# A decoder layer on one core: an order table for attention, a transpose moved to the next half, tile addresses and late loads

## The chip, the cores and the metric

The kernel runs on one core of a Trainium2 chip. A core has five engines that run side by side, each through its own list of instructions in a fixed order: PE (TensorE, the matrix products), DVE (VectorE), ACT (ScalarE), POOL (GpSimd) and SP (SyncE, which only issues transfers here). They wait for each other by semaphores. The metric is the device time of one execution in microseconds (us), lower is better.

## What is computed

One layer for 512 tokens of width 1024, batch 1, in float32. The reference, cut to its skeleton:

```python
h = rmsnorm(x, norm_mix_pre)
z = h @ w_in                      # 1024 x 6704
xr, gr, q, kc, vc, ksl, vsl, kw, vw, g_nsa, gm_rnn, gm_attn = split(z)
y_rnn = rg_lru(causal_conv(xr), ...) * gelu(gr)
kc_c, vc_c = compress(kc, ...), compress(vc, ...)     # 31 blocks of 32 tokens
y_attn = g0 * o_cmp + g1 * o_slc + g2 * o_win         # 16 heads, 4 kv groups, causal, ALiBi
y = sigmoid(gm_rnn) * y_rnn + sigmoid(gm_attn) * y_attn
x = x + rmsnorm(y @ w_out, norm_mix_post)
gate, up = split(rmsnorm(x, norm_ffn_pre) @ ffn_w_gate_up)          # 2 x 2816
x = x + rmsnorm((silu(gate) * up) @ ffn_w_down, norm_ffn_post)
x = x + sigmoid(x @ ple_w_gate + ple_b_gate) * (p @ ple_w_proj)
```

With 512 tokens every block is selected and the window covers all, so the selected and the windowed branch are both full causal attention, with keys and values of their own (branch 0 and 1), beside the compressed branch with its 31 keys.

## The kernel before

Every product is made in three float32r products, high by high, high by low and low by high. A weight block comes by a transfer from SP into `raw`, ACT casts it to `wh`, DVE subtracts to get `wl`; the same is done for every activation (`aTh`, `aTl`) and for the attention weights (`PT`).

The program runs through these stages: the front (norm, transposes to `aTh`/`aTl`, values, the recurrent branch, compression; to about 190 us), attention (about 190 to 455 us), the output projection, the FFN's up part (from about 529 us), its down part, and at the end the gated input embedding (PLE, from about 859 us).

PE's instructions stand in program order. In attention that order is written out by hand. The heads go in eight pairs `p`, and a pair in two halves of the queries, run by `run(p, half, order)` with a string of letters: S a block of scores (PE, bank `sc`, then DVE reduces and copies it to `e` with its minimum `mn`, ACT takes the exponential, and after the last block of a row DVE works out `sm` and POOL scales `e` by it), T a transpose of `e` into a bank `tr` (then an ACT cast and a DVE subtraction make `PT`), M a product of `PT` with the values (bank `pv` in first halves, `mq` in second ones), C the same for the compressed branch. X, Y and Z are the compressed branch of one group of four heads, which is needed by two pairs: X its scores, Y its softmax (`cmp_soft`: DVE steps on `c` and `csm`, the exponential on ACT, and a last product `c*csm` on POOL, line 888), Z its turn (`cmp_turn`: four transposes of `c` into one bank `tr`, two casts `pc` on ACT, line 902, and two subtractions on DVE, line 904). X, Y and Z of the next group stand in the second half of odd pairs (`ODD`). There are two banks of each of `mm`, `sc` and `tr`, so a third user waits until the first one's readers are done.

Digits are fills: one fill is one step (three matmuls) of the projections that lie ready in `attn` (keys `k`, queries `q`, gates `rnn` and `att`). They are what PE does between the dependent steps; there are 224 of them, in one fixed row, and a job's readers on ACT and DVE run when its eighth step is done. `PRO` lists the fills between the steps of the start of attention, before the first pair: `PRO[0]` of them stand ahead of the first scores, `scores(0, 0, 0)`, and `PRO[5]` ahead of `cmp_turn(0)`. The first scores read `KS`, of which one half of the partitions comes by a transfer that POOL issues (line 750).

On the other engines a scheduler sets the order when the program is built, from its own estimate of when each instruction can start. So a change in PE's order changes theirs. `issue_after(x)` says that what is inside may not be put ahead of `x` on its own engine.

The other places: `norm1` takes the reciprocal root on POOL (line 231, a power of a column); POOL fills tables (`toep`, `ctab`, lines 464 to 473) and clears `KC`, `Vz` and `vct` (lines 508 to 510) early in the front, after the first power, `pow0`. In the FFN's up part `gu_act` (line 1157) reads the first product with SiLU into `st`, whose tiles, like `r`, `a` and `s`, come from the pool `ff` at the time of their first use. At the end, `ple_gate_load(ch, k2)` loads, casts and splits one of four blocks `wg` of the PLE gate's weight for one half `ch` of the columns (lines 1209 and 1210); those of `ch` 1 are issued before the third token tile of `ch` 0. Beside them `to_T` (lines 243 and 244) transposes `x1[0]` and `x1[1]` through four banks `sc` into `aTh` and `aTl`, in the middle of the second tile's products.

Of the kernel before, what the change touches and what calls it, by code (L numbers as in the profile page):

```python
# [8 lines left out]
F32 = mybir.dt.float32  # L9
# [7 lines left out]
S, D, KT, TT = 512, 1024, 8, 4  # L17
# [8 lines left out]


HALF0 = "S T S 1 S 2 S T 1 S 2 M S T 1 S T 1 S M M 1 M C 3"
EVEN = "1 T S T 1 C S M T 1 M T 1 S M T T 1 M 1 S T 1 M T 1 M 1 M 3 M"
ODD = "T T X 1 S M T C S 1 Y M S 1 T T M 1 S T M 1 T 2 T M Z M 2 M 1 M 1"  # L30
LAST = "T O O T 1 C 1 O 1 M O T T O O O M 2 M M T W 4 T 2 M T M 1 T 1 M 1 M"
PRO = (22, 5, 0, 2, 1, 10)
TK = (1, 7, 1)
TV = (12, 7, 8, 11)
VP = ()
# [3 lines left out]
def f32(ap):  # L39
    return ap.bitcast(F32)  # L40
# [3 lines left out]
def layer_kernel(ctx, tc, a, out):  # L44
    nc = tc.nc
# [13 lines left out]
    def nm(s):  # L59
        uid[0] += 1  # L60
        return f"{s}{uid[0]}"
# [164 lines left out]
    last = {}  # L226
# [28 lines left out]
    KC = mid.tile([128, NG, 32], F32, name="KC")  # L255
    Vz = mid.tile([128, NG, 2, 128], F32R, name="Vz")
# [3 lines left out]
    vct = mid.tile([64, NG, 4, 32], F32, name="vct")  # L260
# [134 lines left out]
    tp(pg[:, :KT], g_rows, ident[:KT, :KT])  # L395
    kept(nc.vector.tensor_copy(g_col, pg[:, :KT]))
    xn = norm1_halves(x0)
    pow0 = last["pow"].ins
    keep_warm(6)
    with tc.issue_after(last["xn"].ins):  # L400
        vw_first(0, 2, "a")
# [58 lines left out]


    late_pool = ctx.enter_context(ExitStack())
    late_pool.enter_context(tc.issue_after(pow0))
    nc.gpsimd.iota(toep, pattern=[[-1, S]], base=384, channel_multiplier=1,
                   allow_small_or_imprecise_dtypes=True)
    nc.gpsimd.affine_select(toep, toep, pattern=[[-1, S]], base=384, channel_multiplier=1,
# [38 lines left out]
    e2 = e2_stack.enter_context(tc.tile_pool(name="e2", bufs=2, reuse_waits="tile"))  # L505


    nc.gpsimd.memset(KC, 0.0)
    nc.gpsimd.memset(f32(Vz), 0.0)
    nc.gpsimd.memset(vct, 0.0)  # L510
    w2src = [a[n_][0].rearrange("(k p) d -> p k d", p=128) for n_ in ("cmp_k_w2", "cmp_v_w2")]
    for u in range(2):
        nc.sync.dma_start(w2k[:, :, u, :], w2src[0])
# [1 line left out]
    X2s, BLK, PM = {}, {}, {}  # L515
# [340 lines left out]
    def cmp_scores(g):  # L856
        p_ = bank("sc")
        for r in range(4):
            mm(p_[32 * r:32 * r + 32, :], KC[:, g, :], f32(QS[4 * g + r]), start=True, stop=True)
        s1 = ap_.tile([128, S], F32, tag="pvt", name=nm("c1"), bufs=1)  # L860
        nc.scalar.activation(s1, p_, AF.Copy, scale=slcol[:, g:g + 1])
        CG["s1"] = s1

    def cmp_soft(g):
        pt = bank("tr", [128, TT, 4, 32])
        s1 = CG.pop("s1")
        for i in range(TT):
            tp(pt[:, i].rearrange("p r c -> p (r c)"), s1[:, i * 128:(i + 1) * 128], ident)
        s2 = ap_.tile([128, TT, 4, 32], F32, tag="c2", name=nm("c2"), bufs=1)
        for r in range(4):  # L870
            nc.vector.scalar_tensor_tensor(s2[:, :, r, :], ctab, SLOPE[4 * g + r], pt[:, :, r, :],
                                           op0=OP.mult, op1=OP.add)
        mn = ap_.tile([128, TT, 4], F32, tag="cmn", name=nm("cmn"))
        nc.vector.tensor_reduce(mn, s2, axis=AX.X, op=OP.min)
        nc.vector.tensor_scalar(mn, mn, 1.0e30, None, op0=OP.min)
        s2f = s2.rearrange("p i r c -> p (i r) c")
        mnf = mn.rearrange("p i r -> p (i r)")
        nc.vector.tensor_sub(s2f, s2f, mnf[:, :, None].broadcast_to([128, 16, 32]))
        tt = tab if g == 0 else (lambda x: x)
        tt(nc.scalar.activation(s2, s2, AF.Exp, scale=-1.0))  # L880
        sm = ap_.tile([128, TT, 4], F32, tag="csm", name=nm("csm"))
        nc.vector.tensor_reduce(sm, s2, axis=AX.X, op=OP.add)
        nc.vector.tensor_scalar(sm, sm, 1.0e-30, None, op0=OP.max)
        nc.vector.reciprocal(sm, sm)
        gv = gates[:, :, 12 * g:12 * g + 12].rearrange("p i (r b) -> p i r b", b=3)
        nc.vector.tensor_mul(sm, sm, gv[:, :, :, 0])
        smf = sm.rearrange("p i r -> p (i r)")
        nc.gpsimd.tensor_mul(s2f, s2f, smf[:, :, None].broadcast_to([128, 16, 32]))
        CG["s2"] = s2

    def cmp_turn(g):
        pt2 = bank("tr")
        s2 = CG.pop("s2")
        for i in range(TT):
            tp(pt2[:, i * 128:(i + 1) * 128], s2[:, i].rearrange("p r c -> p (r c)"), ident)


        pc = ap_.tile([128, 2, S], F32R, tag="pc", name=nm("pc"), bufs=1)
        lo, hi = slice(0, 64), slice(64, 128)
        hl = list(enumerate(((lo, hi), (hi, lo))))  # L900
        for m, (h_, l_) in hl:
            nc.scalar.copy(pc[h_, m, :], pt2[h_, :])
        for m, (h_, l_) in hl:
            nc.vector.tensor_sub(pc[l_, m, :], pt2[h_, :], f32(pc[h_, m, :]))
        PTc[g] = pc
# [54 lines left out]
    def run(p, half, order):  # L960


        pv_open(p, half)
        if half == 0:
            ss = iter([(p, i, u, (br,)) for i in (2, 3) for u in range(2) for br in range(2)])
        else:
            ss = iter([(p + 1, i, u) for i in (0, 1) for u in range(2)])
        ts, ms, ys = (iter(range(n)) for n in (len(pv_steps(half)), len(pv_steps(half)), KT))
        g = p // 2 + 1
        do = {"S": lambda: scores(*next(ss)), "T": lambda: turn_step(p, half, next(ts)),  # L970
              "M": lambda: pv_step(p, half, next(ms)), "C": lambda: pv_cmp(p, half), "O": lambda: y_split(next(ys)),
              "W": lambda: split_out(), "X": lambda: cmp_scores(g), "Y": lambda: cmp_soft(g), "Z": lambda: cmp_turn(g)}
        for c in order.replace(" ", ""):
            if c.isdigit():
                fill(int(c))
            else:
                do[c]()
        pv_close(p, half)
# [4 lines left out]
    cmp_vz()  # L983
    fill(PRO[0] - 14)
    scores(0, 0, 0)
    fill(PRO[1])
    scores(0, 0, 1)
    fill(PRO[2])
    scores(0, 1, 0)
    fill(PRO[3])  # L990
    cmp_scores(0)
    scores(0, 1, 1)
    fill(PRO[4])
    cmp_soft(0)
    fill(PRO[5])
    cmp_turn(0)
    for p in range(KT - 1):
        run(p, 0, HALF0)
        run(p, 1, (EVEN, ODD)[p % 2])
    p = KT - 1  # L1000
    run(p, 0, HALF0)
# [6 lines left out]
    def split_out():  # L1008
        f_split(NJ + 3, out_hl)
# [131 lines left out]
    NJ2, HS = NF // 2, S // 2  # L1141
    BLK = [tuple(range(b, min(b + 2, NJ2))) for b in range(0, NJ2, 2)]
# [44 lines left out]
    lateb_stack.close()  # L1187
    wo_stack.close()
    ff = ctx.enter_context(tc.tile_pool(name="ff", bufs=1, reuse_waits="tile"))
    for f in range(2):  # L1190
        gu_act(f, *first[f][1])
    for f in range(2, NF):
# [39 lines left out]
    X, Y6, Y7, Z = ([bank(x), bank(y_)] for x, y_ in (("mm", "mm"), ("sc", "sc"), ("tr", "tr"), ("pv", "mq")))  # L1232
# [6 lines left out]
    for b, js in enumerate(BLK):  # L1239
        n = len(js)  # L1240
# [81 lines left out]
    def ple_gate_load(ch, k2):  # L1322
        raw = wraw(wpg[:, 2 * k2:2 * k2 + 2, ch * S:(ch + 1) * S], [128, 2, S], "f", 0)
        if ch == 0:
            hl = ff.tile([128, 2, 2, S], F32R, tag=f"r{k2}", name=nm("wg"))
            h, l = hl[:, 0], hl[:, 1]
        else:
            tags = ("a0", "a1", "a2", "a3", "a4", "s0", "s1", "s2")[2 * k2:2 * k2 + 2]
            h, l = (ff.tile([128, 2, S], F32R, tag=t_, name=nm("wg")) for t_ in tags)
        WG[ch, k2] = split(h, l, raw)  # L1330
# [32 lines left out]
    for ch in range(2):  # L1363
        for i, t in enumerate(ORDER):
            if ch == 0 and i == 2:
                for k2 in range(4):
                    ple_gate_load(1, k2)
            tl = slice(t * 128, (t + 1) * 128)
            pj = bank("tr")
            three(pj, [(pT[0][:, k, tl], pT[1][:, k, tl], WP[ch][0][:, k], WP[ch][1][:, k]) for k in range(2)])  # L1370
            end = ch == 1 and i == TT - 1
            for c0, n_ in ((0, S),) if not end else ((0, S // 2), (S // 2, S // 2)):
                p_ = bank("mm")[:, :n_]
                wc = slice(c0, c0 + n_)
                three(p_, [(aTh[:, k, tl], aTl[:, k, tl], WG[ch, k // 2][0][:, k % 2, wc], WG[ch, k // 2][1][:, k % 2, wc])
                           for k in range(KT)],
                      {1: lambda: to_T(x1[0], 0, "sc"), 5: lambda: to_T(x1[1], 1, "sc")} if (ch, i) == (0, 1) else {})
                z = ff.tile([128, 2, S], F32, tag="st", name=nm("z"), bufs=2)[:, 0, :n_]
                cs = slice(ch * S + c0, ch * S + c0 + n_)
                nc.vector.tensor_add(z, p_, b_g[:, cs])  # L1380
                tab(nc.scalar.activation(z, z, AF.Sigmoid))
                nc.vector.tensor_mul(z, z, pj[:, wc])
                nc.vector.tensor_add(z, z, x1[t][:, cs])
                nc.sync.dma_start(out[0, t * 128:(t + 1) * 128, cs], z)
# [30 lines left out]
```

## Time and profile before

| what | us |
|---|---|
| median of three runs | 927.18 |
| the three runs | 925.63 to 927.47 |
| profiled execution | 926.09 |
| its span in the trace | 924.3 |
| PE busy in it | 903.7 |
| DVE busy | 617.5 |
| ACT busy | 491.5 |
| POOL busy | 128.2 |

The profiled execution has its own time, 926.09 us. Its span, from the first to the last instruction of the trace, is 924.3 us, so 1.8 us lie around it. The engines run side by side, so their busy times overlap. [...]

Matmuls are pipelined: the trace gives one of 512 columns some 0.39 us, and the next starts about 0.23 us after it. PE's time is therefore read from the starts. In the order listings below a row is: the line of the code, the operation, output<-inputs, shape, and a repeat count. All lines after 29 are one higher in the changed kernel.

### The profile page before, as it was taken

The page shows a single profiled execution, that of the slowest core. Times are in us where ns is not written, and L with a number is a line of the kernel's source. Part 1 is how long each engine was busy: PE and PEld are TensorE (multiplying, and loading weights), DVE is VectorE, ACT ScalarE, POOL GpSimd, SP SyncE. Part 2 cuts the span into 40 slices and gives each one's busy share as a digit, 9 for nine tenths or more (in the row PEclk, how much of TensorE's full clock was granted, in tenths as well). Part 3 has the DMA queues.
Part 4 walks back from the last instruction along what each step waited for, and adds up shares of the span by engine and source line. Part 5 has one row for each costly group of instructions (what it writes and reads, how often), then busy time and mean ns, then how long its engine had stood idle before and what let it go on. Part 6 is the DMA issues. An engine that isn't in the chain of part 4 may idle for free.

```text
span 924.3 us, 12453 instructions
## 1 busy us (share of the span) xinstructions
PE 903.7 (98%) x4493; PEld 745.3 (81%) x4493; DVE 617.5 (67%) x1205; ACT 491.5 (53%) x898; POOL 128.2 (14%) x211
## 2 busy tenths in 40 slices
PE   7999999999999999999999999999999999999997
PEld 6978888867878878888888988888888888877786
DVE  6657886967788788886857444434333478898932
ACT  6468868656667667666744322223222245465600
POOL 3001202122243213233303000000000000000100
PEclk9999999999999999999999999999999999999999
DMA  9334345462123111201055123333333345626401
GB/s 298 87 91 114 101 118 147 99 106 66 50 60 78 46 47 46 69 30 62 27 200 160 55 83 91 102 104 91 92 104 101 91 138 186 200 93 224 151 35 46
DMA packets 124206, 94.58 MB, mean 102 GB/s; under 512 B 6168, under 2 KB 107376, under 8 KB 124144
## 3 DMA queue, kind: packets, MB, share of 16 engines
q1 hardware_dynamic: 122976, 91.68, 33.6%
q0 software_dynamic: 1152, 2.10, 1.5%
q8 instruction: 35, 0.57, 0.3%
q14 instruction: 27, 0.22, 0.1%
q10 hardware_dynamic: 16, 0.00, 0.0%
HBM read 89.58 MB, written 2.10 MB: 99 GB/s over the span
## 4 chain that ended last, share of the span: by engine, by line
PE 82%; DVE 9%; ACT 4%; DMA 3%; issue 2%; POOL 0%; SPq 0%; POOLq 0%; ACTq 0%; DVEq 0%
PE mm L96 42%; PE sc L96 24%; PE mq L96 5%; PE tr L96 4%; PE tr L99 4%; PE pv L96 4%; DVE wl L158 1%; DVE PT L923 1%; DMA x<-in_x_dram 1%; DMA KS<-KS 1%; DMA raw<-in_ple_w_gate_dram 1%; DVE aTl L1210 1%; DVE e L837 1%; ACT e L840 1%; DVE T L1222 1%
## 5 line engine op out<-in xcount | busy, mean ns | idle before, releaser
L96 PE MATMUL mm<-aTh,wh 128*128 128x512 f32 (+1 forms) x536 | 211.6, 395 | 0.6 <-ACT st L1157 0.6
L96 PE MATMUL mm<-aTl,wh 128*128 128x512 f32 (+1 forms) x536 | 206.1, 384 | 0.1
L96 PE MATMUL mm<-aTh,wl 128*128 128x512 f32 (+1 forms) x536 | 206.1, 384 | 0.0
L96 PEld LDWEIGHTS mm<-aTh,wl 128*128 128x128 f32 x536 | 100.7, 188 | 20.7
L96 PEld LDWEIGHTS mm<-aTh,wh 128*128 128x128 f32 x536 | 100.9, 188 | 20.2 <-issue 3.4
L84 ACT CAST wh<-raw 128x1024 fp32r<-128x1024 f32 x43 | 45.3, 1054 | 134.4 <-PE mm L96 58.3
L96 PEld LDWEIGHTS mm<-aTl,wh 128*128 128x128 f32 x536 | 101.0, 188 | 16.4 <-DVE aTl L244 0.5
L852 POOL TENSOR_SCALAR e<-e,sm 128x128 f32<-128x128 f32 (+3 forms) x128 | 79.2, 635 | 158.2 <-DVE sm L848 120.0
L85 DVE TENSOR_TENSOR wl<-raw,wh 128x1024 fp32r<-128x1024 f32 x43 | 52.6, 1224 | 67.3 <-ACT wh L84 62.7
L158 DVE TENSOR_TENSOR wl<-raw,wh 128x1024 fp32r<-128x1024 f32 x59 | 73.2, 1244 | 28.9 <-ACT wh L157 24.3
L840 ACT ACTIVATE e<-e,mn 128x128 f32<-128x128 f32 (+3 forms) x128 | 71.5, 560 | 31.3 <-DVE mn L837 20.4
L96 PE MATMUL sc<-aTh,wl 128*128 128x512 f32 (+1 forms) x208 | 79.3, 381 | 0.5 <-DVE wl L158 0.5
L96 PE MATMUL sc<-aTh,wh 128*128 128x512 f32 (+1 forms) x208 | 79.3, 381 | 0.0
L96 PE MATMUL sc<-aTl,wh 128*128 128x512 f32 (+1 forms) x208 | 79.2, 381 | 0.0
L157 ACT CAST wh<-raw 128x1024 fp32r<-128x1024 f32 x59 | 61.6, 1048 | 25.6 <-PE mm L96 20.9
L837 DVE CUSTOM_DVE_ANT_0 e<-sc,toep 128x128 f32<-128x128 f32 (+3 forms) x128 | 59.4, 482 | 19.2 <-PE sc L96 18.6
L923 DVE TENSOR_TENSOR PT<-tr,PT 128x512 fp32r<-128x512 f32 x96 | 56.6, 595 | 14.0 <-ACT PT L922 13.2
L922 ACT CAST PT<-tr 128x512 fp32r<-128x512 f32 x96 | 47.9, 512 | 24.9 <-PE tr L99 20.9
L1043 POOL TENSOR_TENSOR ss<-ss,ss 128x1 f32<-128x1 f32 x8 | 4.9, 615 | 388.0 <-ACT junk L1031 388.0
L96 PE MATMUL sc<-KS,QS 128*128 128x512 f32 (+2 forms) x192 | 54.3, 365 | 2.8 <-DMA KS<-KS 1.9
L99 PE MATMUL tr<-ident,e 128*128 128x128 f32 x320 | 48.5, 272 | 0.0
L99 PEld LDWEIGHTS tr<-ident,e 128*128 128x128 f32 x320 | 39.9, 140 | 8.8
(365 smaller groups left out, 1747.2 us busy)
## 6 DMA issues: line engine op xcount, KB each, us to landing
raw<-in_w_in_dram SPq DMA_DIRECT2D x48, 512.0 KB, 3.8
raw<-in_ffn_w_gate_up_dram SPq DMA_DIRECT2D x44, 512.0 KB, 3.8
raw<-in_ffn_w_down_dram SPq DMA_DIRECT2D x30, 512.0 KB, 4.3
raw<-in_ple_w_gate_dram SPq DMA_DIRECT2D x8, 512.0 KB, 4.1
x<-in_x_dram SPq DMA_DIRECT2D x7, 512.0 KB, 8.4
raw<-in_w_out_dram SPq DMA_DIRECT2D x6, 512.0 KB
raw<-in_cmp_k_w_dram SPq DMA_DIRECT2D x4, 512.0 KB, 3.7
raw<-in_cmp_v_w_dram SPq DMA_DIRECT2D x4, 512.0 KB, 3.9
```

What stands on the lines that cost most here:

```text
L84: nc.scalar.copy(h, raw)
L85: nc.vector.tensor_sub(l, raw, f32(h))
L96: return pe(nc.tensor.matmul(*args, **kw))
L99: return pe(nc.tensor.transpose(*args))
L157: nc.scalar.copy(h, RAW[n])
L158: nc.vector.tensor_sub(l, RAW[n], f32(h))
L837: nc.vector.tensor_tensor_reduce(e[:, br, :], src, toep[:, 384 - 128 * i:S], SLOPE[h], BIG, op0=OP.add, op1=OP.min, accum_out=mn[:, u, br: ...
L840: tt(nc.scalar.activation(e[:, br, :], e[:, br, :], AF.Exp, scale=-1.0, bias=mn[:, u, br:br + 1], accum_out=sm[:, u, br:br + 1]))
L852: nc.gpsimd.tensor_scalar(ev, ev, sm[:, v, br:br + 1], 1.0, op0=OP.mult, op1=OP.mult)
L922: nc.scalar.copy(P[:, 0, :2 * n], pt[:, :2 * n])
L923: nc.vector.tensor_sub(P[:, 1, :2 * n], pt[:, :2 * n], f32(P[:, 0, :2 * n]))
L1210: nc.vector.tensor_sub(l, x, f32(h))
```

## The change

It has four parts, all of them about where things stand; no product, no transfer and no tile is added or taken away.

1. **The order in attention.** `PRO` puts four more fills ahead of the first scores, one fewer between the first and the second scores, and one more ahead of `cmp_turn(0)`; each of the four `EVEN` halves gives one back at its end. Z goes from the second half of odd pairs to the first half of the next pair, behind its first M (`HALFZ`, for pairs 2, 4 and 6).
2. **POOL's tables** and the three clearings are put behind the power of the last token tile, not of the first.
3. **Homes of FFN tiles.** Right when the pool `ff` is opened, a tile of each tag is taken, in a fixed order. Each tag has its address from then on, which is another one than before for the first tile `st`.
4. **The last gate weights** (`ch` 1) may be cast and split only after the last cast and the last subtraction of `to_T`.

```diff
-EVEN = "1 T S T 1 C S M T 1 M T 1 S M T T 1 M 1 S T 1 M T 1 M 1 M 3 M"
-ODD = "T T X 1 S M T C S 1 Y M S 1 T T M 1 S T M 1 T 2 T M Z M 2 M 1 M 1"
+HALFZ = "S T S 1 S 2 S T 1 S 2 M Z S T 1 S T 1 S M M 1 M C 3"
+EVEN = "1 T S T 1 C S M T 1 M T 1 S M T T 1 M 1 S T 1 M T 1 M 1 M 2 M"
+ODD = "T T X 1 S M T C S 1 Y M S 1 T T M 1 S T M 1 T 2 T M M 2 M 1 M 1"
...
-PRO = (22, 5, 0, 2, 1, 10)
+PRO = (26, 4, 0, 2, 1, 11)
...
-    pow0 = last["pow"].ins
...
-    late_pool.enter_context(tc.issue_after(pow0))
+    late_pool.enter_context(tc.issue_after(last["pow"].ins))
...
-    nc.gpsimd.memset(KC, 0.0)
-    nc.gpsimd.memset(f32(Vz), 0.0)
-    nc.gpsimd.memset(vct, 0.0)
+    with tc.issue_after(last["pow"].ins):
+        nc.gpsimd.memset(KC, 0.0)
+        nc.gpsimd.memset(f32(Vz), 0.0)
+        nc.gpsimd.memset(vct, 0.0)
...
-              "W": lambda: split_out(), "X": lambda: cmp_scores(g), "Y": lambda: cmp_soft(g), "Z": lambda: cmp_turn(g)}
+              "W": lambda: split_out(), "X": lambda: cmp_scores(g), "Y": lambda: cmp_soft(g), "Z": lambda: cmp_turn(g - 1)}
...
-        run(p, 0, HALF0)
+        run(p, 0, HALFZ if p and p % 2 == 0 else HALF0)
...
+    ff.tile([128, 2, S], F32, tag="st", name=nm("home"), bufs=2)
+    for j in range(NJ2):
+        if j % 2 == 0:
+            n = len(BLK[j // 2])
+            ff.tile([128, n, 4, HS], F32, tag=f"r{j // 2}", name=nm("home"))
+            ff.tile([128, n, 2, HS], F32, tag=f"a{j // 2}", name=nm("home"))
+        ff.tile([128, 2, 2, HS], F32, tag=f"s{j}", name=nm("home"))
...
-                for k2 in range(4):
-                    ple_gate_load(1, k2)
+                with tc.issue_after(last["Th"].ins), tc.issue_after(last["Tl"].ins):
+                    for k2 in range(4):
+                        ple_gate_load(1, k2)
```

Here is what this does to the order on two engines, at three places.

**DVE in the first softmax of the compressed branch, before** (`c` its weights, `csm` their sums, `wl` a projection weight's low part, `y` the recurrent branch under its gate):

```order
228 L878 TENSOR_TENSOR c_2004<-c_2004,cmn_2009 128x512
229 L158 TENSOR_TENSOR wl_2042<-raw_1930,wh_2041 128x1024
230 L882 TENSOR_REDUCE csm_2014<-c_2004 128x16
231 L771 SCALAR_TENSOR_TENSOR y<-gm_2029,y 128x512
232 L883 TENSOR_SCALAR csm_2014<-csm_2014 128x16
233 L884 RECIPROCAL csm_2014<-csm_2014 128x16
234 L886 TENSOR_TENSOR csm_2014<-csm_2014,gates 128x16
```

The same place on DVE **now**:

```order
228 L159 TENSOR_TENSOR wl_2042<-raw_1920,wh_2041 128x1024
229 L875 TENSOR_REDUCE cmn_2021<-c_2016 128x16
230 L876 TENSOR_SCALAR cmn_2021<-cmn_2021 128x16
231 L879 TENSOR_TENSOR c_2016<-c_2016,cmn_2021 128x512
232 L883 TENSOR_REDUCE csm_2026<-c_2016 128x16
233 L884 TENSOR_SCALAR csm_2026<-csm_2026 128x16
234 L885 RECIPROCAL csm_2026<-csm_2026 128x16
235 L159 TENSOR_TENSOR wl_2079<-raw_2032,wh_2078 128x1024
236 L887 TENSOR_TENSOR csm_2026<-csm_2026,gates 128x16
```

Two splits of weights stand in that stretch where there was one, and the second stands right before the last step, which POOL's product on line 888 waits for.

**PE around Z before**, at the end of pair 1's second half (`c` the compressed weights, `e` the others, `mq` the half's output):

```order
1271 L99 MATMUL tr_2761<-ident,e_2490 128x128
1272 L99 MATMUL tr_2761<-ident,e_2525 128x128
1273 L96 MATMUL mq_2586<-PT_2700,V 128x512 x2
1274 L99 MATMUL tr_2769<-ident,c_2658 128x128 x4
1275 L96 MATMUL mq_2586<-PT_2728,V 128x512 x2
```

**PE around Z now**, in pair 2's first half (`sc` scores, `mm` a fill):

```order
1327 L97 MATMUL pv_2813<-PT_2827,V 128x512 x2
1328 L100 MATMUL tr_2891<-ident,c_2675 128x128 x4
1329 L97 MATMUL sc_2901<-KS_1783,QS_2063 128x512 x2
1330 L100 MATMUL tr_2911<-ident,e_2624 128x128
1331 L100 MATMUL tr_2911<-ident,e_2695 128x128
1332 L100 MATMUL tr_2911<-ident,e_2644 128x128
1333 L100 MATMUL tr_2911<-ident,e_2728 128x128
1334 L97 MATMUL mm_2805<-aTh,wh_2570 128x512
1335 L97 MATMUL mm_2805<-aTl,wh_2570 128x512
1336 L97 MATMUL mm_2805<-aTh,wl_2571 128x512
1337 L97 MATMUL sc_2929<-KS_1783,QS_2065 128x512 x2
1338 L100 MATMUL tr_2934<-ident,e_2695 128x128
```

Z has moved some 50 instructions of PE further down. The second transpose behind it (1338) takes the bank that Z had filled.

**DVE in the last stage, before** (`z` a tile of the result, `wg` a gate weight's low part, `aTl` the low part of the transposes of `x1[0]` and `x1[1]`):

```order
1107 L1380 TENSOR_TENSOR z_7853<-mm_7828,b_g 128x512
1108 L1210 TENSOR_TENSOR wg_7934<-raw_7931,wg_7933 128x1024
1109 L244 TENSOR_TENSOR aTl<-sc_7870,aTh 128x4x128
1110 L1210 TENSOR_TENSOR wg_7940<-raw_7937,wg_7939 128x1024
1111 L1382 TENSOR_TENSOR z_7853<-z_7853,tr_7821 128x512
1112 L244 TENSOR_TENSOR aTl<-sc_7877,aTh 128x4x128
1113 L1383 TENSOR_TENSOR z_7853<-z_7853,x_5027 128x512
1114 L244 TENSOR_TENSOR aTl<-sc_7896,aTh 128x4x128
```

DVE there **now**:

```order
1114 L1390 TENSOR_TENSOR z_7877<-mm_7852,b_g 128x512
1115 L1392 TENSOR_TENSOR z_7877<-z_7877,tr_7845 128x512
1116 L245 TENSOR_TENSOR aTl<-sc_7894,aTh 128x4x128
1117 L1393 TENSOR_TENSOR z_7877<-z_7877,x_5027 128x512
1118 L245 TENSOR_TENSOR aTl<-sc_7901,aTh 128x4x128
1119 L245 TENSOR_TENSOR aTl<-sc_7920,aTh 128x4x128
1120 L245 TENSOR_TENSOR aTl<-sc_7927,aTh 128x4x128
1121 L1219 TENSOR_TENSOR wg_7952<-raw_7949,wg_7951 128x1024
```

The four splits `wg` stand behind all four `aTl`, and the second step of `z`, which needs ACT's sigmoid, stands ahead of the first of them; on ACT the sigmoid stands ahead of all four casts `aTh`, where before it stood behind the first.

## Rows read from the trace of the kernel before

**Rows 1.** The page: each engine's busy time with its share of the span.

```profile
PE 903.7 (98%) x4493; PEld 745.3 (81%) x4493; DVE 617.5 (67%) x1205; ACT 491.5 (53%) x898; POOL 128.2 (14%) x211
```

**Rows 2.** Waits of PE: line <- what it waited for: us, times, longest.

```profile
PE tr L99 <- POOL c L888: 2.1, 3, 0.8
...
PE sc L99 <- DVE aTl L244: 1.6, 1, 1.6
...
PE mq L96 <- DVE PT L923: 0.9, 3, 0.5
PE sc L96 <- DVE mn L837: 0.9, 2, 0.5
PE mm L96 <- ACT st L1157: 0.6, 1, 0.6
```

**Rows 3.** Timeline of PE, 191 to 211 us: start, duration, [idle before <- releaser].

```profile
193.62 0.47 PE L96 MATMUL sc<-KS,QS 128*128 128x256 f32 x2 [1.93 <-DMA KS<-KS]
...
210.12 0.66 PE L99 MATMUL tr<-ident,c 128*128 128x128 f32 x4 [0.81 <-POOL c L888]
```

**Rows 4.** Timeline of DVE, then of POOL, in the first softmax.

```profile
205.50 1.45 DVE L158 TENSOR_TENSOR wl<-raw,wh 128x1024 fp32r<-128x1024 f32 x1 [0.34 <-ACT wh L157]
...
208.69 0.18 DVE L886 TENSOR_TENSOR csm<-csm,gates 128x16 f32<-128x16 f32 x1
...
209.02 1.05 POOL L888 TENSOR_TENSOR c<-c,csm 128x512 f32<-128x512 f32 x1 [1.27 <-DVE csm L886]
```

**Rows 5.** Timeline of PE, ACT and DVE around Z at the end of pair 1.

```profile
272.60 0.66 PE L99 MATMUL tr<-ident,c 128*128 128x128 f32 x4 [1.61 <-DVE sm L848]
273.01 0.48 PE L96 MATMUL mq<-PT,V 128*128 128x512 f32 x1
...
273.29 1.17 ACT L902 CAST pc<-tr 64x512 fp32r<-64x512 f32 x2 [1.04 <-PE tr L99]
...
274.49 1.39 DVE L904 TENSOR_TENSOR pc<-tr,pc 64x512 fp32r<-64x512 f32 x2 [0.46 <-ACT pc L902]
```

**Rows 6.** Timeline of PE, DVE and ACT in pair 2's first half, where Z will stand.

```profile
284.18 0.64 PE L96 MATMUL sc<-KS,QS 128*128 128x512 f32 x2
284.65 0.60 PE L99 MATMUL tr<-ident,e 128*128 128x128 f32 x4
...
286.24 0.38 PE L99 MATMUL tr<-ident,e 128*128 128x128 f32 x2
...
284.70 0.66 DVE L837 CUSTOM_DVE_ANT_0 e<-sc,toep 128x512 f32<-128x512 f32 x1
...
285.46 0.72 ACT L840 ACTIVATE e<-e,mn 128x512 f32<-128x512 f32 x1 [1.86 <-DVE sm L848]
```

**Rows 7.** Timeline of ACT at the start of the FFN's up part.

```profile
528.18 1.28 ACT L1157 ACT_TABLE_LOAD   x1
529.96 1.09 ACT L1157 ACTIVATE st<-mm 128x512 f32<-128x512 f32 x2 [0.49 <-PE sc L96]
```

**Rows 8.** Timeline of POOL, then DVE, then ACT, in the last stage.

```profile
863.87 0.55 POOL L231 TENSOR_TENSOR rstd<-rstd,mhalf 128x1 f32<-128x1 f32 x1 [0.70 <-DVE rstd L230]
...
866.61 1.46 POOL L231 TENSOR_TENSOR rstd<-rstd,mhalf 128x1 f32<-128x1 f32 x1 [0.70 <-DVE rstd L230]
...
869.44 0.68 DVE L1380 TENSOR_TENSOR z<-mm,b_g 128x512 f32<-128x512 f32 x1
...
873.50 0.68 DVE L244 TENSOR_TENSOR aTl<-sc,aTh 128x512 fp32r<-128x512 f32 x1
...
871.49 0.63 ACT L1381 ACTIVATE z<-z 128x512 f32<-128x512 f32 x1
```

**Rows 9.** Timeline of DVE in the front: two halves of a norm, the first beside POOL's tables; `norm1`.

```profile
6.38 0.77 DVE L322 TENSOR_SCALAR xn<-x,rstd 128x512 f32<-128x512 f32 x1 [0.74 <-POOL rstd L320]
...
7.14 0.47 DVE L322 TENSOR_SCALAR xn<-x,rstd 128x512 f32<-128x512 f32 x1
...
20.09 2.47 DVE L335 SCALAR_TENSOR_TENSOR xn<-x,rstd,gpre 128x1024 f32<-128x1024 f32 x2
```

## The prediction

> **What bounds the kernel now.** The page comes first [rows 1]: PE is busy in 98% of the span, the next engine, DVE, in 67%. No row of the change takes a product away, so all that can be won is time in which PE stands still, some 20 us in all, and all that can be lost is a new stop of PE. So the second view is the list of PE's waits [rows 2], and the third the timeline around each of those that the change touches [rows 3 to 8]. What the reader is to see: the stops are short, 0.2 to 2 us, and spread over the whole program; each has one releaser; most lie in attention, where PE's order is a hand-written table and each step waits for a chain through DVE, ACT and POOL. A stop printed as idle time is some 0.16 us short of the loss from start to start (matmuls are pipelined and their ends modelled); I add it where I price a stop from its row. The clock was full throughout, so it plays no part.
>
> **First scores.** PE waits 1.93 us for the transferred half of KS [rows 3], 2.09 with the pipeline's share. Four more fills ahead of them are 4 x 3 matmuls at 0.23 us, 2.8 us. They cover the wait with 0.7 us to spare, and they are no new work: the row of fills is fixed, and each of the four EVEN halves gives one back. Term: -2.1. What is late next is the first turn of the compressed weights. PE waits 0.81 us there for POOL's product on line 888 [rows 3], which runs 1.05 us after the last step on `csm` [rows 4]. By the order now, DVE has one more weight split ahead of that last step, 1.45 us in the nearest row [rows 4]; some 0.34 us of it fits into an idle gap that DVE has there now, so POOL's product is about 1.1 us later. PE comes later as well: eleven plus the other fills make 51 against 47, so 2.8 us more work less the 2.1 saved, 0.7 us. The wait grows by about 0.5 us. Bounds: -0.8 (it goes, if the split does not delay `csm`) and +1.0. Term: +0.5.
>
> **First half of pair 0.** Two stops of PE for a score bank, 0.9 us of idle time in all [rows 2], come from DVE running late with the scores behind the compressed softmax. With PE 1.2 us later (0.7 and 0.5) against the same DVE, I take away the second and leave the first: -0.65, bounds -1.2 and 0.
>
> **Z in the second halves.** Three stops go: 1.61 us at the end of pair 1 [rows 5], and two behind POOL's product in the odd pairs after it, which with the first turn's 0.81 make 2.1 [rows 2], so 1.3. With 0.16 or so each, 3.4 us. That is the gain with nothing in its place.
>
> **Z in the first halves.** Its input has long been ready there, so Z itself does not wait. What waits is the second transpose behind it, as there are two `tr` banks and it wants the one that Z filled. The trace shows that chain once in the open [rows 5]: Z starts at 272.60, ACT's two casts start 0.69 us later and take 1.17, DVE's two subtractions end at 274.49 + 1.39 = 275.88. The bank is free 3.28 us after Z's start, at the earliest. PE's work up to that transpose: Z itself 0.41 (272.60 to 273.01), then a score, a transpose, a fill and a score. The same row of steps stands at 284.18 to 286.24 [rows 6], 2.06 us. So PE is there 2.47 us after Z's start and waits 0.8. Three times: +2.4. From below nothing, if the next steps have slack that I don't see; from above 3.4 each, in the rival on Z's bank.
>
> **Queues behind Z and the fills.** ACT and DVE are in-order. Behind DVE's two subtractions on `pc` stands the eviction of the next transpose, so the M that uses it may come too early for its `PT`; keys, gates and weight splits have moved by one to four fills against the steps, and stand ahead of evictions in pair 1's and 3's second halves and pair 2's first and second. I count four such places. Each is worth nothing up to about half of the 1.39 us that the two subtractions take [rows 5]; I take 0.3 each: +1.2, bounds 0 and 2.8. On the other side, two `PT` stops at the ends of the EVEN halves of pairs 2 and 6, most of the 0.9 us in [rows 2], go, because the last `PT` subtraction now stands ahead of a weight split there and not behind it: -0.95, bounds -0.95 and 0.
>
> **Homes.** PE's stop for `st` is 0.6 us [rows 2]. The SiLU starts at 529.96 although its table was there at 528.18 + 1.28 = 529.46 [rows 7]: it waits 0.49 us for PE's last read of a weight at the address that its output takes. The tile now has another address, so the SiLU starts when the table is there: -0.5, bounds -0.7 and 0. [...]
>
> **Last gate weights.** PE waits 1.56 us for `aTl` [rows 2], the second subtraction of the four, at 873.50 to 874.18 [rows 8]. Three splits of 1.2 us stand in front of it on DVE. Without them one would expect the whole wait back. But ACT's sigmoid, whose table load takes 1.28 us here too, now stands ahead of the first cast, and DVE's step on `z` behind it ahead of the first subtraction. Walked through: POOL's power takes 0.55 us and not 1.46, since no split runs beside it [rows 8]; so DVE's first step on z, which ended at 869.44 + 0.68 = 870.12, ends 0.91 earlier, at 869.2. The table load (1.28) and the sigmoid (0.63) follow to 871.15, then DVE's second step on z, the first subtraction, the third step and the second subtraction, four of 0.68 less their overlap of 0.07 each, to some 873.7. Term: -0.45, bounds -1.7 and +0.4. The splits themselves are first used a whole column half later.
>
> **POOL's tables later.** They no longer run beside the first norm, where DVE's first half took 0.77 us and the same form 0.47 later, but behind the fourth power, beside the last two norms, 2 x 1.24 us from 20.09 [rows 9]. PE waits 0.2 us for those already, so what they lose is on the path. I take +0.35, about the 0.30 that the first half lost; bounds -0.3 (the earlier norm gets its time back) and +0.75. [...] The nearest row is the half that took 0.77 us beside the tables and 0.47 without [rows 9]; at that ratio the two would lose 1.6 us, and the sum below would be 1.2 us smaller.
>
> **The sum.** -2.1 + 0.5 - 0.65 - 3.4 + 2.4 + 1.2 - 0.95 - 0.5 - 0.45 + 0.35 = -3.6 us. The profiled execution took 926.09 us (924.3 of span, 1.8 around), so it would be 922.5. That execution lies 1.1 us under the median of the three runs, 927.18; from the median, 923.6. I give that. A measurement of this kernel tells about 0.2%, 1.85 us, from no change, so faster means under 925.3 and slower over 929.0.
>
> **Rivals.** *Nothing new stands up.* Z's bank and the queues behind it have slack, since PE's first half has fills to both sides; the terms +2.4 and +1.2 fall away: -7.2, 920.0. For it speaks that the trace shows no stop on a `tr` bank anywhere now; against it the chain of 3.28 us, which is measured.
>
> *The gain is given back in the queues.* The second split ahead of `csm` costs 1.0 in place of 0.5, the four evictions 2.8 in place of 1.2, as each comes behind a full instruction: -3.6 + 0.5 + 1.6 = -1.5, 925.7, no change that can be told. For it speaks that the change shifts every key, gate and split against the steps, and each of these engines takes its work in a fixed order.
>
> *Z's bank decides, and the kernel is slower.* ACT's two casts may stand with an exponential between them, and DVE's subtractions stand behind the next score's reduction. Then the bank waits for that score: Z 0.41 and the score's 0.64, the reduction 0.66, the exponential 0.72 [rows 6], the second cast 0.58 and the subtractions 1.39 [rows 5] end 4.4 us after Z's start in place of 3.28, and with a weight split of 1.45 us ahead of the reduction [rows 4] 5.85. PE waits 3.4 us in each of the three halves, 7.8 more than in my sum: +4.2, 931.4. The point from which it decides: the sum is zero at 2.0 us for each half, and slower by 0.2% from 2.6. For it: DVE has that order. Against it: in the order now an exponential stands between the casts in one of the three halves only, and it is that of an earlier score.
>
> *A part does nothing*: the SiLU still ends with the table, and the stop in the last stage only moves from `aTl`'s splits to the sigmoid. That takes 0.95 from the sum, -2.65, 924.5, inside the forecast's own range.
>
> **How the numbers follow.** Forecast (-1.85 to -5.5 us): 0.46. Nothing new: 0.17. Given back: 0.27. Z's bank: 0.10. Faster is the first two, 0.63; same 0.27; slower 0.10. The time is the forecast's, 923.6. The forecast's own range is 921.7 to 925.3. The range for 8 in 10 leaves out the slower case and the lower half of the case with nothing new: from 919.9 up to 927.7, where the queues' bounds and the tables' +0.75 come together.
>
> **What would show it.** In the trace after: no wait of the first scores on KS; the first turn's wait at 1.0 to 1.6 us on line 888; no wait of PE on `c` later; waits of a transpose on DVE's `pc` (0.8 us, three times) in the first halves of pairs 2, 4 and 6; the SiLU right behind its table load; the last `aTl` stop at about 1.1 us with the sigmoid ahead of it; `norm1`'s two DVE steps over 1.24 us. I am wrong if the waits on `pc` are missing (then the lower end holds) or above 2 us (then the gain is gone), or if the first turn's wait takes most of the first scores' gain.

## The result

The changed kernel takes 935.24 us (median of four runs, 934.43 to 936.79), the kernel before beside it 926.40 us. The ratio is 1.0097 with a 95% interval of 1.0078 to 1.0117: slower by 9 us. The prediction was 923.6 us, faster. Both the sign and the size were missed, and the time lies outside the range of 919.9 to 927.7.

The profiled execution has a span of 933.7 us against 924.3. The page says at once that no work was added, only standing still: the counts of instructions are those of [rows 1], and so are the busy times but for PE's. Of PE's 3.8 us more, 1.7 is the clock and about 1.1 the end of the pipeline at seven more stops, as shown below; 1.0 is not accounted for.

```profile
PE 907.5 (97%) x4493; PEld 746.6 (80%) x4493; DVE 617.9 (66%) x1205; ACT 491.6 (53%) x898; POOL 127.9 (14%) x211
```

The waits of PE in attention alone (188 to 480 us; line <- what it waited for: us, times, longest):

```profile
PE sc L97 <- DVE mn L838: 4.6, 4, 2.2
PE tr L100 <- DVE pc L905: 3.1, 3, 1.7
PE tr L100 <- DVE PT L924: 2.0, 2, 1.3
PE tr L100 <- POOL e L853: 1.9, 4, 0.9
PE tr L100 <- POOL c L889: 1.7, 1, 1.7
PE mq L97 <- DVE PT L924: 1.4, 2, 1.1
PE pv L97 <- DVE PT L924: 0.5, 1, 0.5
```

They add up to 15.2 us. The same view of the kernel before holds 7.4: of [rows 2] the rows on `c`, `PT` and `mn`, the 1.93 us of [rows 3] and the 1.61 of [rows 5]. The wait for KS is gone, as was forecast, and so are the stops of Z at the ends of the odd pairs' halves. In their place stand the three waits on `pc` that the prediction priced at 2.4 us (they are 3.1), and, not priced at anything like their size, stops for a score's reduction, for `PT` and for `e`: 10.4 us of them where the kernel before had 1.8. Of these 10.4, 0.65 us are two stops that the kernel before had as well, so 9.8 us are new.

The longest stands at the start of pair 2. The timeline of PE, then DVE, then ACT there (start, duration, [idle before <- releaser]):

```profile
278.46 0.51 PE L97 MATMUL sc<-KS,QS 128*128 128x384 f32 x2
...
279.16 0.60 PE L97 MATMUL sc<-KS,QS 128*128 128x384 f32 x2
...
282.65 0.78 PE L97 MATMUL sc<-KS,QS 128*128 128x384 f32 x2 [2.19 <-DVE mn L838]
...
278.58 1.23 DVE L159 TENSOR_TENSOR wl<-raw,wh 128x1024 fp32r<-128x1024 f32 x1 [2.72 <-ACT wh L158]
279.72 1.40 DVE L749 TENSOR_TENSOR KS<-mm,KS 64x512 fp32r<-64x512 f32 x2
281.15 0.85 DVE L954 TENSOR_TENSOR att<-mq,pvt 64x256 f32<-64x256 f32 x2
282.03 0.56 DVE L838 CUSTOM_DVE_ANT_0 e<-sc,toep 128x384 f32<-128x384 f32 x1
...
277.50 1.05 ACT L158 CAST wh<-raw 128x1024 fp32r<-128x1024 f32 x1 [2.34 <-PE mm L97]
278.45 1.17 ACT L746 CAST KS<-mm 64x512 fp32r<-64x512 f32 x2
279.64 0.58 ACT L952 COPY pvt<-mq 64x512 f32<-64x512 f32 x1
```

The reader is to see a queue. The job of the keys that is under way ends three fills earlier against the steps than before, which is just at the seam between two pairs. ACT takes the weight's cast, the keys' two casts and the seam's own copy `pvt` one behind the other. DVE takes what follows from them, the weight's split, the keys' two subtractions and the two sums `att`, 3.5 us in all. Behind them stands the reduction of pair 2's first score. Its input, the score that PE began at 278.46, was ready by about 279.0; the reduction starts at 282.03. PE has two `sc` banks, has filled both, and stands for 2.2 us. In the kernel before, DVE came to the first reduction at 278.02; the split and the two subtractions stood behind the pair's first three reductions:

```profile
278.02 0.56 DVE L837 CUSTOM_DVE_ANT_0 e<-sc,toep 128x384 f32<-128x384 f32 x1
...
280.96 1.23 DVE L158 TENSOR_TENSOR wl<-raw,wh 128x1024 fp32r<-128x1024 f32 x1 [0.83 <-ACT wh L157]
...
282.64 1.41 DVE L748 TENSOR_TENSOR KS<-mm,KS 64x512 fp32r<-64x512 f32 x2
```

### The profile page after: what moved, and what is told of

Same layout as the page of the kernel before. It is cut to its first block, busy times and chain, and to the rows that moved or that the text cites. A ratio compares the mean times of both kernels' runs of the same rounds, so it can differ in the third digit from the quotient of the medians.

```text
span 933.7 us, 12455 instructions
## 1 busy us (share of the span) xinstructions
PE 907.5 (97%) x4493; PEld 746.6 (80%) x4493; DVE 617.9 (66%) x1205; ACT 491.6 (53%) x898; POOL 127.9 (14%) x211
```

## The experiments

All are shown as the ratio to the kernel before on the same chip, with its 95% interval.

**e1_fills: the fills alone.** The first question was which half of part 1 does it.

```diff
-... 1 M 1 M 3 M"            # EVEN
-PRO = (22, 5, 0, 2, 1, 10)
+... 1 M 1 M 2 M"            # EVEN
+PRO = (26, 4, 0, 2, 1, 11)
```

> The kernel before with the new numbers of fills alone: PRO (26, 4, 0, 2, 1, 11) and one fill less at the end of each EVEN half; Z stays in the second halves. Theory A (the shift of the fills: job ends come up to four fills earlier against the steps, so that splits of KS, QS and weights stand on DVE and ACT ahead of evictions and reductions): the stops that the changed kernel shows at 230, 259, 269, 280 and 319 us appear here too, some 7 us of them, the three stops of Z at the odd halves' ends stay; the first scores give 2 back and the first turn costs 0.9 more; 5 to 9 us slower than before. Theory B (Z's new place: its bank chain holds up all that follows): none of these stops, -1 to -2 us against before.

**e2_z: Z's new place alone.** HALFZ for pairs 2, 4 and 6, ODD without Z, and the fills of before.

```diff
-ODD = "... 2 T M Z M 2 M 1 M 1"
+HALFZ = "S T S 1 S 2 S T 1 S 2 M Z S T 1 S T 1 S M M 1 M C 3"
+ODD = "... 2 T M M 2 M 1 M 1"
```

> The kernel before with Z's new place alone (HALFZ, ODD without Z), the numbers of fills as before. Theory A: the three stops of Z go (-3.4 us) and three stops of a transpose on pc come (+3.6 us, as in the changed kernel), little else: -1 to +1.5 us. Theory B: the stops at 259 to 425 us of the changed kernel come here, 6 to 10 us slower.

**e3_rest: the other three parts alone.** The changed kernel with the four tables of the order as before.

```diff
-PRO = (26, 4, 0, 2, 1, 11)
+PRO = (22, 5, 0, 2, 1, 10)
...
-        run(p, 0, HALFZ if p and p % 2 == 0 else HALF0)
+        run(p, 0, HALF0)
```

> The changed kernel with its order in attention undone: POOL's tables, the homes and the last gate weights alone. Both theories: attention as before; the front gains up to 1 us, the stop for st 0.4, the last stage 0.5: 1 to 2 us faster than before, which a measurement barely tells.

Measured: the fills alone 1.0121 (1.0097 to 1.0145), 936.6 us; Z alone 1.0025 (1.0010 to 1.0040); the rest alone 0.9981 (0.9967 to 0.9996). The fills alone are slower by 11 us, more than the whole change, and more than the 5 to 9 that theory A gave them. The waits of PE in attention with the fills alone have the changed kernel's rows on `mn`, `e`, `c` and `PT` at the top:

```profile
PE sc L96 <- DVE mn L837: 4.7, 4, 2.3
PE tr L99 <- POOL e L852: 3.2, 5, 1.4
PE tr L99 <- POOL c L888: 2.3, 2, 1.7
PE tr L99 <- DVE PT L923: 2.0, 2, 1.3
```

So the loss comes from the shift of the fills, as theory A had it, and not from Z's new place. Theory B falls. Z alone cost 2.3 us, where theory A said -1 to +1.5, and its trace tells why. This is pair 2's first half, PE, then DVE, then ACT:

```profile
286.80 0.41 PE L100 MATMUL tr<-ident,e 128*128 128x128 f32 x2 [1.89 <-DVE pc L905]
...
285.26 1.39 DVE L905 TENSOR_TENSOR pc<-tr,pc 64x512 fp32r<-64x512 f32 x2 [1.14 <-ACT pc L903]
...
282.88 0.58 ACT L903 CAST pc<-tr 64x512 fp32r<-64x512 f32 x1 [1.21 <-PE tr L100]
283.81 0.72 ACT L841 ACTIVATE e<-e,mn 128x512 f32<-128x512 f32 x1 [0.35 <-DVE sm L849]
284.65 0.58 ACT L903 CAST pc<-tr 64x512 fp32r<-64x512 f32 x1
```

An exponential stands between the two casts, and waits itself for DVE; the subtractions wait for the second cast, the transpose for the subtractions. The three waits on `pc` come to 4.5 us of idle time there, where the stops of Z that went were 2.9. This is the rival on Z's bank in a mild form: Z's move by itself gains nothing.

**e4_back: the four fills given back at once,** in pair 0's first half, so that from its second half on every job ends at the step at which it ended before.

```diff
+HALFP = "S T S 1 S 2 S T 1 S 2 M S T 1 S T 1 S M M M C"
...
-        run(p, 0, HALF0)
+        run(p, 0, HALF0 if p else HALFP)
```

> The kernel before with PRO (26, 4, 0, 2, 1, 11), the four fills taken back at once, in pair 0's first half (its last C 3 and one more fill), EVEN as before: from pair 0's second half on every job ends at the step at which it ended before. Theory A: the stops of e1_fills from 230 us on are missing; what the first scores gain (2.1) is less the first turn's 0.9 and what the thinner first half costs (0 to 1.5): -1.2 to +0.5 us against before, and 5 us or more faster than e1_fills. Theory B: the same time as e1_fills.

Measured: 1.0014 (0.9999 to 1.0029), 8.9 us under e1_fills, which shared its runs of the kernel before. None of the later stops of e1_fills is left; the three of Z are back as before. But the thinner half has one new stop, and it is as long as the one it was meant to save:

```profile
PE tr L100 <- POOL e L853: 2.5, 1, 2.5
```

It stands at the first transposes of pair 0's second half. This is DVE, then POOL, ahead of it:

```profile
225.05 1.39 DVE L764 SCALAR_TENSOR_TENSOR QS<-mm,QS 64x512 fp32r<-64x512 f32 x2 [0.15 <-ACT QS L760]
...
227.64 0.16 DVE L849 TENSOR_TENSOR sm<-sm,gates 128x2 f32<-128x2 f32 x1
...
228.05 1.36 POOL L853 TENSOR_SCALAR e<-e,sm 128x512 f32<-128x512 f32 x2 [1.54 <-issue]
```

Two things meet. With four fills fewer, PE comes to these transposes at 225.78 and not at 227.23 us. And the last step on `sm` stands behind the two subtractions on QS and the sums `att`: it starts at 227.64, and POOL's last scaling of `e` at 228.05, where the kernel before had them at 224.81 and 225.46. So part of this stop is again a queue on DVE; the run does not tell how much the thinner half would cost without it. At 1.3 us above the kernel before, the run also lies above what was expected, -1.2 to +0.5.

**e5_defer, e6_defer_epi and e9_pin: PE's order as in e1_fills to the last matmul, but the readers later.** A job's readers on ACT and DVE, and the splits of later weights, are handed over as many fills later as the fills are ahead (4 from pair 0 on, then 3, 2, 1), which should give them the place of before against the steps. In e6_defer_epi only the readers are. In e9_pin the scheduler may not put either ahead of the step in front of them.

```diff
 def fill(n):
     for _ in range(n):
         next(filler[0], None)
+        nfill[0] += 1
+        flush()        # runs what is held, once nfill - shift has reached its mark
...
-                f_split(n + 2)
+                held(lambda n=n: f_split(n + 2))
...
-            EPI[what[0]](*what[1:])(p_)
+            held(lambda what=what, p_=p_: EPI[what[0]](*what[1:])(p_), 1)
```

> The order of PE is that of e1_fills to the last matmul, but what ACT and DVE do for the fills (a job's readers, and the split of a later weight block) is handed to them as many fills later as the fills are ahead, 4 in pair 0, then 3, 2, 1: their place against scores, turns and evictions is that of the kernel before. Queue theory (the early readers and splits stand on ACT and DVE in front of what PE waits for): the stops at 231, 269, 282, 320 and 368 us of e1_fills go, Z's three stay; 924 to 927 us, 9 to 12 less than e1_fills. Rival (PE's own order: fewer or other matmuls between dependent steps): the stops stay, 935 us or more.

> As e5_defer, but only the jobs' readers (KS, QS, the gates) are handed over later; the splits of weights come as early as in e1_fills. If the readers do the damage: within 2 us of e5_defer. If the splits do: within 2 us of e1_fills. I expect the readers to have the larger part: 926 to 931 us.

> As e5_defer, and each of the readers and splits handed over may now also not be put ahead of the last step of attention (a score's reduction and exponential, a turn's cast and subtraction, the softmax of the compressed weights) that stands before it. Queue theory: what e5_defer kept of the loss (4.5 us) is where the scheduler still put them ahead, so it falls further: 924 to 927 us, with the first turn's stop at 0.3 to 1 us and not 1.83. Rival (the rest is PE's own order): 929 to 930 us as e5_defer.

Measured: e5_defer 1.0047 (1.0030 to 1.0063), e6_defer_epi 1.0084 (1.0067 to 1.0101), e9_pin 1.0020 (1.0008 to 1.0032). With the same matmuls in the same order the kernel takes 936.6, 933.3, 929.7 or 927.4 us, by where ACT's and DVE's readers and splits stand; the kernel before took 925.2 to 925.5 beside them. So most of the 11 us is not PE's own order. The expectations for e5_defer (924 to 927 us) and e6_defer_epi (926 to 931) were too good, and readers and splits each make about half of what e5_defer won back, not mostly the readers. For a part of what e5_defer kept, the scheduler had put them ahead all the same: the ban of e9_pin takes another 2.3 us away. In attention e5_defer kept these three among its waits, of which the stop on `mn` at pair 2's first score is 0.9 us and not 2.3:

```profile
PE tr L100 <- POOL c L905: 2.3, 2, 1.7
PE tr L100 <- DVE sm L865: 2.3, 2, 1.6
PE sc L97 <- DVE mn L854: 2.1, 4, 0.9
```

and e9_pin these, where the stop at pair 2's first score is gone and the first turn's stop fell from 1.7 to 0.5:

```profile
PE tr L100 <- POOL e L876: 1.9, 3, 1.4
PE tr L100 <- POOL c L913: 1.9, 3, 0.7
PE tr L100 <- DVE sm L872: 1.6, 1, 1.6
PE sc L97 <- DVE mn L860: 1.2, 2, 0.6
```

**e10_pin0: the control.** The ban of e9_pin on the kernel before, whose fills and Z stay, with nothing handed over later.

> The control to e9_pin: the kernel before, its fills and Z as they were, with the same ban on being put ahead. It tells what the ban costs or gives by itself. I expect 924 to 928 us.

Measured: 1.0046 (1.0030 to 1.0062). The ban by itself costs some 4 us, where none or little was expected (924 to 928 us); which readers it holds up stays open. Under the same ban the new fills, with their readers handed over later (e9_pin), are 2.7 us faster than the old ones: with the readers kept in their place, four fills ahead of the first scores are a gain. The prediction's terms for them (-2.1, +0.5 and -0.65) make 2.25; but the 2.7 is the net of several stops that moved, so the nearness may be luck. Beside this, e11_rest_pin put the other three parts on e9_pin.

> e9_pin with the tables, homes and last gate weights of the changed kernel: 1.5 to 2 us less than e9_pin by the sum of e3_rest's gain; by the queue theory 922 to 925 us.

Measured: 1.0004 (0.9991 to 1.0016), 1.2 us under e9_pin in the medians and not the 1.5 to 2 expected; no change against the kernel before that can be told.

**e7_zlate and e8_all: Z behind the last transpose.** If the bank is what makes Z dear, it should be free where no transpose follows.

```diff
-HALFZ = "S T S 1 S 2 S T 1 S 2 M Z S T 1 S T 1 S M M 1 M C 3"
+HALFZ = "S T S 1 S 2 S T 1 S 2 M S T 1 S T 1 Z S M M 1 M 3 C"
```

> e3_rest (tables, homes, last gate weights; fills as before) with Z in the first halves of pairs 2, 4 and 6, but behind the last transpose there, with the half's three last fills moved ahead of C: no transpose wants Z's bank within 3.3 us, and pc has some 4 us until C. Bank theory: neither the stops of Z at the odd halves' ends nor those on pc: 3 to 4 us less than e3_rest, 920 to 923 us. If Z in a first half costs by the work that it adds to ACT and DVE there: stops of the following steps, 1 to 3 us more than that.

> e7_zlate with the new numbers of fills and the readers and splits handed over later as in e5_defer. By the queue theory the first scores' gain comes on top: 1 to 2 us less than e7_zlate, 919 to 922 us. By its rival 8 us or more above e7_zlate.

Measured: e7_zlate 0.9995 (0.9980 to 1.0011), e8_all 1.0023 (1.0014 to 1.0033). The expectations were missed by 2 and by 5 us; e7_zlate's time is the one that its rival gave, by which Z's work costs the steps that follow. Both, and e12_even0 below, have the other three parts of the change in them, so they are to be held against e3_rest. In e7_zlate the waits on `c` at the odd halves and those on `pc` are gone, and what is late next took their place, mostly a `PT` early in the half that follows:

```profile
PE mq L97 <- DVE PT L924: 3.5, 5, 1.1
```

It was 0.9 us in [rows 2]. C now stands at the very end of the half, so the half's output is copied and summed (`pvt`, `att`) in the next half, ahead of that `PT` on DVE. The work of Z and C on ACT and DVE has to stand somewhere, and at each of the three places tried an M or a T waits behind it.

**e12_even0: the fills given back in pair 0's second half**, on top of e3_rest.

```diff
+EVEN0 = "1 T S T 1 C S M T 1 M T 1 S M T T 1 M 1 S T 1 M T M M 1 M"
...
-        run(p, 1, (EVEN, ODD)[p % 2])
+        run(p, 1, (EVEN, ODD)[p % 2] if p else EVEN0)
```

> e3_rest with the new PRO, where the four fills are all given back in pair 0's second half (EVEN without its last 1 fill before three M's and one of the 3), so that from pair 1 on every job ends where it did before; no readers are handed over later. Theory of the shift: no stop beyond pair 0 that e3_rest doesn't have; first scores -2.1, first turn +0.9, pair 0's first half -0.65, its second half +0.5 to +2 as in e1_fills and for thinner cover: -1.3 to +0.2 us against e3_rest. Rival (the first scores' gain is not to be had without the loss): 3 us or more above e3_rest.

Measured: 0.9993 (0.9981 to 1.0004). There is no later stop beyond pair 0, as the theory of the shift said, and no gain over e3_rest, whose ratio is lower by 0.0012, about 1.1 us (-1.3 to +0.2 was expected; the two intervals overlap). The wait on KS is gone, 2.3 us in e3_rest; the first turn's stop grew by 0.9, and one for a `PT` of 1.1 us came in pair 0's second half. The lowest ratio of all is e3_rest's, which leaves the order in attention alone: 0.9981 of the kernel before, about 1.8 us.

## Why the prediction was wrong, step by step

**The step that failed: the queues behind Z and the fills.** The prediction counted four places and took 0.3 us for each, 1.2 in all, with 2.8 as the upper bound, from half of what one pair of subtractions takes. The new stops for `mn`, `PT` and `e` are 9.8 us of idle time. Two things were wrong with how the term was sized. A place was priced by one instruction, while at a seam several stand behind each other (1.23 + 1.40 + 0.85 us at pair 2): the four places that it counted cost 6.4 us, over twice its upper bound. And places were left out: 3.4 us stand elsewhere, the most of it 1.71 us at the start of pair 3, where a weight split, two steps on a gate, the sums `att` and a `PT` stand ahead of the second reduction, and 1.11 in pair 0's second half. The sum of what stands ahead of the awaited instruction could have been read from the order before the run. In pair 1's second half it is the keys' other job: its two subtractions on KS (1.41 us) stand ahead of the reductions and of the `PT` that a transpose waits for; in the kernel before they started at 269.82 and 270.72 us, behind those reductions.

```profile
266.58 1.41 DVE L749 TENSOR_TENSOR KS<-mm,KS 64x512 fp32r<-64x512 f32 x2
...
270.59 0.66 PE L100 MATMUL tr<-ident,e 128*128 128x128 f32 x4 [1.34 <-DVE PT L924]
...
321.54 0.61 PE L97 MATMUL sc<-KS,QS 128*128 128x384 f32 x2 [1.71 <-DVE mn L838]
```

The two `PT` stops at the ends of EVEN halves did go, as the term of -0.95 had it, but the one of 1.11 us in pair 0's took their place.

**The clock, which "plays no part", did.** In the kernel before the granted clock was 1.00 up to PE's last matmul at 918.8 us. In the changed kernel it fell to 0.50 behind the stop at pair 2, for some 3.4 us: matmuls of 512 columns start 0.43 us apart there (283.23, 283.66, 284.08), not 0.23. Six of them and two pairs of shorter ones run so: some 1.7 us, which the page books as PE's busy time. e1_fills has the same fall behind the same stop (granted 0.50 from 286 to 288 us). Three stretches of the changed kernel (us, PE, PEld, DVE, ACT and POOL busy, granted clock, DMA share, GB/s):

```profile
281.00:282.60 1.60, 0.00 (x0) 0.00 (x0) 1.52 (x6) 0.00 (x0) 0.93 (x2) 1.00 0.97 262
282.60:284.00 1.40, 1.35 (x4) 1.25 (x5) 1.40 (x4) 1.00 (x3) 0.00 (x0) 0.62 1.46 272
284.00:286.00 2.00, 2.00 (x6) 1.53 (x5) 0.15 (x2) 1.01 (x4) 0.00 (x0) 0.50 0.80 119
```

**First scores: right.** The wait for KS is gone. **The first turn: right in kind, mis-sized by a third of a microsecond.** The second split stands where the order had it, and the product on POOL comes 1.6 us later; PE waits 1.67 us, start to start 1.83, where 0.97 plus 0.5 was forecast. DVE, POOL and PE of the changed kernel:

```profile
209.24 1.16 DVE L159 TENSOR_TENSOR wl<-raw,wh 128x1024 fp32r<-128x1024 f32 x1
210.32 0.17 DVE L887 TENSOR_TENSOR csm<-csm,gates 128x16 f32<-128x16 f32 x1
...
210.64 1.05 POOL L889 TENSOR_TENSOR c<-c,csm 128x512 f32<-128x512 f32 x1 [2.85 <-DVE csm L887]
...
211.74 0.44 PE L100 MATMUL tr<-ident,c 128*128 128x128 f32 x2 [1.67 <-POOL c L889]
```

**First half of pair 0: right.** One of the two stops is left, 0.37 us of idle time (0.53 start to start).

**Z: the mechanism right, the price low.** Its three old stops went, and the second transpose behind it waits on `pc` three times: 0.72, 1.69 and 0.71, 3.1 us in the changed kernel against the 2.4 forecast, and 4.5 with the fills of before.

**Homes and last gate weights: right, within 0.1 us or so. Tables: dearer in the forecast than on the path.** SiLU starts at 539.66, when its table is there (538.37 + 1.28 = 539.65), so the stop for `st` is gone (ACT). In the last stage the sigmoid ends at 881.0 with the casts behind it, and two stops of 0.44 and 0.55 us, not one of 1.1, replace the 1.56 of [rows 2]. POOL's power ahead of them took 0.55 us (at 876.42) with no split beside it on DVE, where the 1.46 of [rows 8] had one beside it, 1.22 us from 866.45. `norm1` takes 2.83 us where [rows 9] had 2.47, +0.36 with POOL's tables now beside it (from 20.02 us on), and the first half-norm 0.49 where it had 0.77. On the path less of it is seen: DVE stood 0.37 us ahead of the kernel before at the last step before the first half-norm (5.11 for 5.48), when no table had been filled in either, and is still 0.24 ahead behind `norm1` (22.55 for 22.79), so the two together cost about 0.13 and not 0.35.

```profile
538.37 1.28 ACT L1158 ACT_TABLE_LOAD   x1
539.66 1.09 ACT L1158 ACTIVATE st<-mm 128x512 f32<-128x512 f32 x2
```

```profile
880.39 0.63 ACT L1391 ACTIVATE z<-z 128x512 f32<-128x512 f32 x1
...
882.40 0.66 PE L100 MATMUL sc<-ident,x 128*128 128x128 f32 x4 [0.44 <-DVE aTl L245]
883.60 0.66 PE L100 MATMUL sc<-ident,x 128*128 128x128 f32 x4 [0.55 <-DVE aTl L245]
```

```profile
6.01 0.49 DVE L323 TENSOR_SCALAR xn<-x,rstd 128x512 f32<-128x512 f32 x1 [0.74 <-POOL rstd L321]
...
19.80 2.83 DVE L336 SCALAR_TENSOR_TENSOR xn<-x,rstd,gpre 128x1024 f32<-128x1024 f32 x2
```

In both places the norm with POOL's tables beside it took longer, 0.77 us against 0.49 and 2.83 against 2.47. The other half of [rows 9], at 7.14 us, had a table beside it as well, POOL's 0.82 us on `toep` from 7.26, and took 0.47; in the changed kernel, with POOL idle beside them, the two halves take 0.49 and 0.48. The runs do not show which of POOL's steps lengthen which of DVE's. The ratio of the two halves (0.77 to 0.47), applied to the two norms, would have given 1.6 us, and the row shows 0.36. In e3_rest the three parts together measure 1.8 us (0.4 to 3.1), where the sum had 0.6; the interval does not part the two.

**The rivals.** "The gain is given back in the queues" named the right mechanism, and gave the queues 2.8 us where they had 9.8 and the clock's 1.7 to give. Its chance was 0.27, and its price was capped by the same bounds as the term's. No rival had the queues as the cause of a slower kernel; the one that ended slower, Z's bank, was the wrong place. Nearly all that the prediction listed under what would show it came true (no wait on KS, the waits on `pc`, the SiLU, `norm1`) while the time did not: none of these signs looked at the queues. The sum of attention, made again from what was measured, is: printed waits +7.8 (15.2 for 7.4), the pipeline's share of 0.16 us for each of seven stops more, 1.1, and the clock's 1.7, together 10.6, where the prediction's terms for attention make -3.0. The starts on PE agree: it comes to the first scores 0.5 us early, counted without the four fills, and to the first product of the output projection at 490.88 and not 480.70, so attention grew by 10.7. Behind it 0.8 came back; the span grew by 9.4.

**What stays open.** e9_pin is still 2 us above the kernel before. Its control shows that the ban costs 4, but not which readers the ban holds up. And other shifts than this one were tried at two points only (all given back in pair 0's first or second half).

## What to carry to other kernels

Filler work in a hand-written order is not neutral: each of its blocks ends in readers and splits on other engines, and moving a block by a few steps moves these in front of what the bound engine waits for. Before such a move is priced, take from the new order, for each instruction that the bound engine waits for, all that stands ahead of it from the moment its input is there, and sum it; a place's bound is that sum, not one instruction. Fills that cover one wait are taken from another place, and what was won at the first can be lost there (here 2.1 us at the first scores, and a stop of 2.5 in the half that had to give the fills back). And a stop can cost more than its length: here behind one of 2.2 us the granted clock was 0.50 for 3.4 us, which cost another 1.7.

## What the runs showed of the hardware

The granted clock did not fall behind every long stop. In the changed kernel and in e1_fills it fell from 1.00 to 0.50 behind the stops of 2.2 and 2.3 us at pair 2, and was back at 1.00 some 3.4 us later. Behind the single stops of 1.93 us in the kernel before, of 1.89 in e2_z and of 2.5 in e4_back it stayed at 1.00. It fell near shorter ones too: in the front of e3_rest and of e8_all, which have a stop of 1.0 and one of 0.9 us there, it was 0.50 from about 11.8 and 11.4 us on, while the kernel before, with one of 1.03 at the same place, and the changed one, with 0.96, kept 1.00. The runs do not show what makes the difference; at pair 2, PE had also stood for 1.3 us some 10 us before in both kernels.
